# A fused NSA + DSA decoder layer on one Trainium2 core: another price for transfers in the order, own raw buffers for the MLP, one tile for two tables

## The chip, the core and the metric

The kernel runs on one core of a Trainium2 chip. The metric is the device time of one launch in microseconds. Engines are called as the profile calls them: PE (TensorE; PEld is its weight load), DVE (VectorE), ACT (ScalarE), POOL (GpSimd) and SP (SyncE, which here only issues transfers).

## What is computed

One decoder layer over 512 tokens of width 1024, in float32. One projection feeds two groups of heads, which are mixed side by side and mapped back together:

```
h = rms_norm(x, norm_gain)                        # 512 x 1024
q_n, kc, vc, ks, vs, kw, vw, gates, z_n, q_d, k_d, v_d, qi, ki, wi, z_d = split(h @ w_in)
# group A (8 heads, 2 kv heads)
qn, ks, kw = rope(rms_norm(.))                    # per head, width 64
kc_cmp = rope(rms_norm(compress(kc)));  vc_cmp = compress(vc)
   # compress: blocks of 32 tokens, stride 16 -> flat(2048) @ w1(2048 x 256) + b1 -> silu -> @ w2(256 x 64)
o_n = g0*attend(qn, kc_cmp, vc_cmp) + g1*attend(qn, selected blocks of ks, vs) + g2*attend(qn, kw, vw)
# group B (8 heads, 2 kv heads): an indexer picks 128 keys for each query
score = sum_h wi[h] * relu(rope(qi)[h] @ rope(ki)^T)
keep  = top_k(score, 128), causal
o_d   = attend(rope(rms_norm(q_d)), rope(rms_norm(k_d)), v_d) on the kept keys
out   = x + concat(o_n * silu(z_n), o_d * silu(z_d)) @ w_out
```

There are two compress MLPs, one for keys and one for values; each has its own `w1` of 2048 x 256.

## The kernel before, in words

**Precision.** A float32 matrix product is made of three products of rounded parts: a weight tile is loaded raw, ACT casts it to its high part and POOL (or DVE) subtracts that from the raw tile for the low part (`split`, L355 to L357). So each weight piece of 256 KB costs a transfer, an ACT cast (L356) and a subtraction (L357), and then PE multiplies high by high, high by low and low by high (L390, L400).

**Raw pieces.** `load_raw` (L349) takes a tile from a ring and issues the transfer on SP (L352). All weights share the ring "raw" of four buffers (`RAWB`), the sixteen pieces of `w1` that `load_w1` (L733) fetches among them; a transfer into a buffer waits until the cast and the subtraction of the piece that held it are done. In names, `raw_w103` is piece 3 of the keys' `w1`, `raw_w110` piece 0 of the values'; `w1h`, `w1l` are their parts. Weights of the projection are B (indexer and small ones), C (compressed keys and values), Q, D and Z.

**Stages.** Projections for blocks of tokens or columns (L390, L400, L479); the indexer (L672 to L706: PE multiplies the four heads' queries of a block of 128 tokens with the keys at L689, into PSUM banks of the tag S, of which there are two; ACT takes the relu in place at L691; DVE adds the heads up at L693 and L695 and finds the largest 128 of a row in sixteen rounds of L700 and L701); the compress MLP (`chunk_C`, and `hidden`: 32 matmuls at L776, then DVE L781, L782 and L784 with ACT's tanh L783 between them; `hid0` is the keys', `hid1` the values'); norms and rope of queries and keys (L531 and L536, with tables from `tables`, L517 to L522); attention, for blocks of 128 tokens from the last to the first (scores L1010, row maximum on DVE L982, exponential on ACT L987, transposes L1029, product with the values L1040; `P_n301` and `s_n301` are of block 3, its first rows); the gates, and the output product (L1219).

**What sets the order.** The program is written as interleaved generators, but the engines' queues are not in that order. `set_order` (L98) reads all instructions, works out who depends on whom (ring buffers too), gives every one a cost (L115) and every hand-over between engines a latency (`LATENCY`, L71), and lists each engine's queue anew: `turns` runs through the program backward for due times and forward for an order, eight rounds long, and the best order by its own clock is fixed as a chain per engine. So the five queues run strictly in the order that this gives, SP's too. Numbers that steer it: `SOON` (how far ahead an instruction may be waited for that is more urgent), `PORT` (weight of the port that DVE and POOL share, when it is late), `SPARE` (added to the latency of every hand-over to PE) and the price of a transfer (L272 to L282). When a transfer is priced in the forward run, it lands 650 after its issue or when the transfer before is done, whichever is later, and its length (128 partitions times the bytes of a row, by 360) after that.

Of the kernel before, what the change touches and what calls it, by code (L numbers as in the profile page):

```python
# [9 lines left out]
F32 = mybir.dt.float32  # L10
# [6 lines left out]
S, D, HD = 512, 1024, 64  # L17
NT = S // 128
# [65 lines left out]
    ("SP", "PE"): 900, ("SP", "DVE"): 950, ("SP", "Activation"): 900, ("SP", "Pool"): 950,  # L84
}

URGENT, SOON = 3000, 300
PE_URGENT, PE_SOON = 200, 60
ROUNDS = 8

# [2 lines left out]
LO_DVE = {"C": range(2)}  # L93

WBUFS = 4
PORT = 10

TURN = {"Activation": 125, "DVE": 118}  # L98

CHOICE = 0.0  # L100

SPARE = 200

HURRY = {}

# [3 lines left out]
def set_order(tc):  # L109
# [66 lines left out]
    for k, i in enumerate(insts):  # L176
        acc = []
        for w, ap in aps(i):
# [4 lines left out]
            end = off + sum((n - 1) * st for st, n in dims[1:] if st > 0) + 1  # L183
# [17 lines left out]
    for bufs, names in ring.values():  # L201
        names.sort(key=lambda name: int(name.rsplit("_", 1)[1]))
        for x, name in enumerate(names):
# [3 lines left out]
            if x:  # L207
                j = used[names[x - 1]][0]
# [11 lines left out]
    costs = [cost(i, e) for i, e in zip(insts, eng)]  # L220
# [9 lines left out]
    def turns(due, back=False):  # L230
# [5 lines left out]
        idle = defaultdict(float)  # L236
# [13 lines left out]
        for _ in range(count):  # L250
# [21 lines left out]
            end = idle[e] = start[k] + costs[k][0] + more  # L272
            if port[k]:
                idle["port"] = end
            if by[k] == "SP":
                if back:
                    idle["transfers"] = max(idle["transfers"], start[k]) + costs[k][1]
                    end = max(end, idle["transfers"]) + 650
                else:
                    end = max(end + 650, idle["transfers"]) + costs[k][1]  # L280
                    idle["transfers"] = end
                    there = there[1:] + [end + 900]  # L282
            if back:
# [2 lines left out]
            for q in to[k]:  # L286
                left[q] -= 1
                j, i = (q, k) if back else (k, q)
# [20 lines left out]
def tile_hybrid_layer(ctx, tc, xT, x, ng, win, gains, peT, w1, b1, w2, wout, cst, out):  # L309
# [39 lines left out]
    def load_raw(src, shape, name, where=None):  # L349
        tag, bufs = where or ("raw", RAWB)  # L350
        v = wp.tile(shape, F32, tag=tag, name=name, bufs=bufs)
        nc.sync.dma_start(v, src)  # L352
        return v
# [162 lines left out]

    def tables(j, name):  # L517
        gn = gns[:, j, None, :]
        c, s = (work.tile([128, NT, HD], F32, tag="tab" + x, name="tab" + x, bufs=3) for x in "cs")
        nc.gpsimd.tensor_tensor(c, cosd, gn[:, :, :HD].to_broadcast([128, NT, HD]), op=ALU.mult)  # L520
        nc.gpsimd.tensor_tensor(s, sind, gn[:, :, HD:].to_broadcast([128, NT, HD]), op=ALU.mult)
        return c, s  # L522
# [209 lines left out]

    def load_w1(kv):  # L733
        for j in range(8):
            raw = load_raw(w1[:, kv, 2 * j:2 * j + 2, :], [128, 2, 256], f"raw_w1{kv}{j}")
            if j % 2 == 0:
                pair = [w1_tile(kv, j, x) for x in range(2)]
            w1t[kv, j] = [v[:, 2 * (j % 2):2 * (j % 2) + 2] for v in pair]
            split(raw, *w1t[kv, j], nc.gpsimd)
# [659 lines left out]
```

## Time and profile before

| | us |
|---|---|
| three runs: median (lowest, highest) | 316.26 (315.95, 316.64) |
| the profiled execution: its time | 316.42 |
| the profiled execution: span of the core | 314.6 |
| busy in that span: PE, PEld | 306.6, 258.9 |
| busy in that span: DVE, ACT, POOL | 261.1, 242.3, 234.1 |

The span runs from the first to the last instruction that the profile shows; 1.8 us of the profiled execution lie outside of it. The granted clock of PE is 1.00 in all stretches, which is the upper of its two levels, 2.4 GHz. All durations below are of this one profiled execution. Busy time of PE counts a matmul up to its modelled end, and matmuls overlap, so the time that PE loses is read from the starts of its instructions and not from its share.

### The profile page before, as it was taken

The numbers are of one execution on the slowest core, as the hardware profiler recorded it, in microseconds if no ns is written. First come the engines' busy times: TensorE is split into PE (matmuls) and PEld (weight loads), VectorE is DVE, ScalarE is ACT, GpSimd is POOL, SyncE is SP. The second block draws the span as 40 slices with busy tenths as digits, with TensorE's granted clock in tenths as the row PEclk, the third lists the DMA queues.
The fourth block names the chain that finished last, engine by engine and source line by source line (L and its number), as shares of the span: only waits on it lengthen the run. The fifth ranks groups of instructions, "written<-read, shape, count | busy, mean of one in ns | idle before, by whom it ended". The sixth has DMA issues, their size and how long they took to land.

```text
span 314.6 us, 6043 instructions
## 1 busy us (share of the span) xinstructions
PE 306.6 (97%) x1681; PEld 258.9 (82%) x1681; DVE 261.1 (83%) x797; ACT 242.3 (77%) x794; POOL 234.1 (74%) x416
## 2 busy tenths in 40 slices
PE   8999999899999999999999999999999999999995
PEld 5998888789877888888887888888888888888885
DVE  4996624689999999999999999999999999886501
ACT  5971666778999899899999989883379998996500
POOL 2079989799885499995899889766877995667500
PEclk9999999999999999999999999999999999999999
DMA  7990365656510033320040044042435242003011
GB/s 259 417 322 4 98 172 144 173 163 170 165 40 1 0 83 92 97 85 3 3 133 3 4 134 134 2 124 72 135 106 163 70 151 76 20 0 133 2 67 67
DMA packets 21249, 32.16 MB, mean 102 GB/s; under 512 B 5664, under 2 KB 8480, under 8 KB 21216
## 3 DMA queue, kind: packets, MB, share of 16 engines
q1 hardware_dynamic: 21216, 31.78, 33.2%
q8 instruction: 13, 0.21, 0.3%
q14 instruction: 20, 0.16, 0.2%
HBM read 29.04 MB, written 2.47 MB: 100 GB/s over the span
## 4 chain that ended last, share of the span: by engine, by line
PE 81%; ACT 7%; DMA 4%; POOL 3%; issue 2%; DVE 1%; SPq 1%; POOLq 0%; DVEq 0%
PE out L1219 14%; PE z L400 14%; PE D L390 7%; PE on L1040 7%; PE s_n L1010 6%; PE T_n L1029 6%; PE Q L390 5%; PE I L479 5%; DMA raw_w<-in_w_dram 4%; PE C L400 3%; PE od L1040 3%; PE T_d L1029 3%; PE s_d L1010 3%; POOL w1l L357 2%; PE I L443 1%
## 5 line engine op out<-in xcount | busy, mean ns | idle before, releaser
L987 ACT ACTIVATE P_n<-P_n,arena 128x416 f32<-128x416 f32 (+9 forms) x64 | 33.5, 525 | 3.3 <-DVE arena L982 2.8
L1000 POOL TENSOR_SCALAR P_n<-P_n,arena 128x416 f32<-128x416 f32 (+7 forms) x64 | 30.4, 493 | 1.1
L982 DVE CUSTOM_DVE_ANT_0 P_n<-s_n,arena 128x416 f32<-128x416 f32 (+9 forms) x64 | 30.3, 489 | 0.5
L1031 DVE TENSOR_TENSOR ptl<-T_n,pth 128x512 fp32r<-128x512 f32 x40 | 27.4, 684 | 1.8 <-ACT pth L1030 1.3
L1010 PE MATMUL s_n<-kn,arena_r 128*128 128x288 f32 (+12 forms) x116 | 28.3, 328 | 0.5 <-DVE arena_r L621 0.5
L700 DVE MAX8 m<-scores 128x8 f32<-128x512 f32 (+2 forms) x48 | 26.6, 554 | 0.5
L1029 PE MATMUL T_n<-arena,P_n 128*128 128x128 f32 x160 | 26.9, 272 | 0.0
L701 DVE MATCH_REPLACE8 scores<-m,scores 128x512 f32<-128x512 f32 (+2 forms) x48 | 26.1, 544 | 0.1
L400 PE MATMUL z<-hThi,whi_Z 128*128 128x512 f32 x64 | 25.7, 404 | 0.0
L400 PE MATMUL z<-hThi,wlo_Z 128*128 128x512 f32 x64 | 25.3, 398 | 0.0
L400 PE MATMUL z<-hTlo,whi_Z 128*128 128x512 f32 x64 | 25.2, 397 | 0.0
L1030 ACT CAST pth<-T_n 128x512 fp32r<-128x512 f32 x40 | 23.4, 587 | 1.9 <-PE T_n L1029 1.4
L1010 PEld LDWEIGHTS s_n<-kn,arena_r 128*128 128x128 f32 x116 | 20.7, 188 | 4.6 <-DVE arena_r L621 0.7
L1029 PEld LDWEIGHTS T_n<-arena,P_n 128*128 128x128 f32 x160 | 20.3, 140 | 4.8 <-POOL P_n L1000 0.2
L1219 PE MATMUL out<-wohi,mx 128*128 128x512 f32 (+1 forms) x72 | 23.9, 378 | 0.0
L1219 PE MATMUL out<-whi_wo,mx 128*128 128x512 f32 (+1 forms) x72 | 23.6, 379 | 0.0
L357 POOL TENSOR_TENSOR wlo_Z<-raw_Z,whi_Z 128x512 fp32r<-128x512 f32 x16 | 20.4, 1295 | 3.6 <-ACT whi_Z L356 3.5
L390 PE MATMUL Q<-whi_Q,hThi 128*128 128x256 f32 (+1 forms) x64 | 22.4, 349 | 0.0
L357 POOL TENSOR_TENSOR w1l<-raw_w,w1h 128x512 fp32r<-128x512 f32 x16 | 20.5, 1289 | 2.4 <-DMA raw_w<-in_w_dram 1.3
L390 PE MATMUL Q<-whi_Q,hTlo 128*128 128x256 f32 (+1 forms) x64 | 22.2, 347 | 0.0
L390 PE MATMUL Q<-wlo_Q,hThi 128*128 128x256 f32 (+1 forms) x64 | 21.8, 340 | 0.0
L1040 PE MATMUL on<-ptl,arena_r 128*128 128x512 f32 x48 | 20.0, 417 | 0.0
(264 smaller groups left out, 1099.2 us busy)
## 6 DMA issues: line engine op xcount, KB each, us to landing
raw_w<-in_w_dram SPq DMA_DIRECT2D x16, 256.0 KB, 3.1
raw_Z<-in_win_dram SPq DMA_DIRECT2D x16, 256.0 KB, 3.0
wor<-in_wout_dram SPq DMA_DIRECT2D x16, 256.0 KB, 2.8
raw_Q<-in_win_dram SPq DMA_DIRECT2D x12, 256.0 KB, 2.8
raw_D<-in_win_dram SPq DMA_DIRECT2D x8, 256.0 KB, 3.0
xres<-in_x_dram SPq DMA_DIRECT2D x8, 256.0 KB, 2.8
out_dram<-xres SPq DMA_DIRECT2D x7, 256.0 KB, 2.0
xw<-in_xT_dram SPq DMA_DIRECT2D x2, 860.0 KB, 8.8
```

What stands on the lines that cost most here:

```text
L357: engine.tensor_tensor(lo, raw, hi.bitcast(F32), op=ALU.subtract)
L390: nc.tensor.matmul(out_ps, a[:, k, tsl], b, start=(k == 0 and b is hi and a is hT["hi"]), stop=(k == KB - 1 and a is hT["lo"]))
L400: nc.tensor.matmul(out_ps, b[:, csl], a[:, k, :], start=(k == 0 and b is hi and a is hT["hi"]), stop=(k == KB - 1 and b is lo))
L700: nc.vector.max(m8, sc)
L982: nc.vector.tensor_tensor_reduce(P, src_, mask, u.r[:, b:b + 1], 3e38, op0=ALU.add, op1=ALU.min, accum_out=m[:, b:b + 1])
L987: nc.scalar.activation(P, P, AF.Exp, bias=m[:, b:b + 1], scale=-1.0, accum_out=l[:, b:b + 1])
L1000: nc.gpsimd.tensor_scalar(Pb, Pb, l[:, bb:bb + 1], 1.0 if u.gate is not None else 0.5, op0=ALU.mult, op1=ALU.mult)
L1010: nc.tensor.matmul(p, q[0][:, b], k[:, x], start=(x == 0), stop=(x == 1))
L1029: nc.tensor.transpose(p[:, h * 128:(h + 1) * 128], u.P[:, h, j * 128:(j + 1) * 128], ident)
L1031: nc.vector.tensor_tensor(pl, p, ph.bitcast(F32), op=ALU.subtract)
L1040: nc.tensor.matmul(o, u.v[j], pp, start=(u.first and j == 0 and x == 0), stop=(end and x == 1))
L1219: nc.tensor.matmul(p, a, b[:, csl], start=(k == 0 and b is hi and a is mx[0]), stop=(k == 7 and a is mx[1]))
```

## The change

Five places change, and no instruction is added or taken out; each engine has as many as before.

- The forward price of a transfer (L280): where the transfers before are done, it now lands later by 0.7 of its own length.
- `SOON` from 300 to 400, `PORT` from 10 to 8, `SPARE` from 200 to 250.
- The sixteen raw pieces of `w1` get a ring of their own, "raww", of four buffers. The ring "raw" serves the other weights alone.
- The two rope tables of a chunk, two tiles in two rings of three, become the halves of one tile in one ring of three.

```diff
--- before.py
+++ after.py
@@ -84,7 +84,7 @@
     ("SP", "PE"): 900, ("SP", "DVE"): 950, ("SP", "Activation"): 900, ("SP", "Pool"): 950,
 }
 
-URGENT, SOON = 3000, 300
+URGENT, SOON = 3000, 400
 PE_URGENT, PE_SOON = 200, 60
 ROUNDS = 8
 
@@ -93,13 +93,13 @@
 LO_DVE = {"C": range(2)}
 
 WBUFS = 4
-PORT = 10
+PORT = 8
 
 TURN = {"Activation": 125, "DVE": 118}
 
 CHOICE = 0.0
 
-SPARE = 200
+SPARE = 250
 
 HURRY = {}
 
@@ -277,7 +277,7 @@
                     idle["transfers"] = max(idle["transfers"], start[k]) + costs[k][1]
                     end = max(end, idle["transfers"]) + 650
                 else:
-                    end = max(end + 650, idle["transfers"]) + costs[k][1]
+                    end = max(end + 650 + 0.7 * costs[k][1], idle["transfers"]) + costs[k][1]
                     idle["transfers"] = end
                     there = there[1:] + [end + 900]
             if back:
@@ -516,7 +516,8 @@
 
     def tables(j, name):
         gn = gns[:, j, None, :]
-        c, s = (work.tile([128, NT, HD], F32, tag="tab" + x, name="tab" + x, bufs=3) for x in "cs")
+        tab = work.tile([128, 2, NT, HD], F32, tag="tab", name="tab", bufs=3)
+        c, s = tab[:, 0], tab[:, 1]
         nc.gpsimd.tensor_tensor(c, cosd, gn[:, :, :HD].to_broadcast([128, NT, HD]), op=ALU.mult)
         nc.gpsimd.tensor_tensor(s, sind, gn[:, :, HD:].to_broadcast([128, NT, HD]), op=ALU.mult)
         return c, s
@@ -732,7 +733,7 @@
 
     def load_w1(kv):
         for j in range(8):
-            raw = load_raw(w1[:, kv, 2 * j:2 * j + 2, :], [128, 2, 256], f"raw_w1{kv}{j}")
+            raw = load_raw(w1[:, kv, 2 * j:2 * j + 2, :], [128, 2, 256], f"raw_w1{kv}{j}", where=("raww", 4))
             if j % 2 == 0:
                 pair = [w1_tile(kv, j, x) for x in range(2)]
             w1t[kv, j] = [v[:, 2 * (j % 2):2 * (j % 2) + 2] for v in pair]
```

Since the queues follow from the prices and from the buffers, all five are listed anew. Three places, before and after (after the change, lines from the tables on have a number higher by one, L622 for L621).

SP's queue from the last piece of B on, before: the piece of B, three small loads (the MLP's positions, `b1` and `w2`), the eight pieces of the keys' `w1`, then (not shown) pieces of Q.

```order
L352 DMA raw_B7_370<-in_win_dram 128x512
L710 DMA arena_72<-in_peT_dram 128x32
L712 DMA b1r_394<-in_b1_dram 64x512
L714 DMA arena_72<-in_w2_dram 128x256
L352 DMA raw_w100_505<-in_w1_dram 128x512
L352 DMA raw_w101_511<-in_w1_dram 128x512
L352 DMA raw_w102_515<-in_w1_dram 128x512
L352 DMA raw_w103_521<-in_w1_dram 128x512
L352 DMA raw_w104_525<-in_w1_dram 128x512
L352 DMA raw_w105_531<-in_w1_dram 128x512
L352 DMA raw_w106_535<-in_w1_dram 128x512
L352 DMA raw_w107_541<-in_w1_dram 128x512
```

The same place after the change:

```order
L352 DMA raw_B7_370<-in_win_dram 128x512
L352 DMA raw_w100_505<-in_w1_dram 128x512
L352 DMA raw_w101_511<-in_w1_dram 128x512
L352 DMA raw_w102_515<-in_w1_dram 128x512
L352 DMA raw_w103_521<-in_w1_dram 128x512
L713 DMA b1r_394<-in_b1_dram 64x512
L715 DMA arena_72<-in_w2_dram 128x256
L352 DMA raw_w104_525<-in_w1_dram 128x512
L352 DMA raw_Q10_957<-in_win_dram 128x512
L352 DMA raw_Q11_961<-in_win_dram 128x512
L352 DMA raw_w105_531<-in_w1_dram 128x512
L352 DMA raw_Q12_967<-in_win_dram 128x512
```

The first four pieces of `w1` stand straight behind the last piece of B, and the next four alternate with pieces of Q, which now come out of the other ring.

ACT's queue around the indexer of block 3 (`idx30` to `idx33`; `sq` are squares for the norms of projected B, `kix` the indexer's keys, `FS` the MLP's input, L855 a copy of values), before:

```order
L542 ACTIVATE sq_903,ss_kb_547<-B_3_876 128x64
L356 CAST w1h10_1045<-raw_w110_1043 128x512
L764 CAST FS1_495<-ff10_497 128x8x2x31
L542 ACTIVATE sq_910,ss_kb_547<-B_3_876 128x64
L356 CAST w1h10_1045<-raw_w111_1049 128x512
L542 ACTIVATE sq_912,ss_kb_547<-B_3_876 128x64
L691 ACTIVATE idx30_570<-idx30_570 128x512
L691 ACTIVATE idx31_581<-idx31_581 128x512
L356 CAST w1h12_1055<-raw_w112_1053 128x512
L855 ACTIVATE arena_r_73<-B_3_876,arena_72 128x4x64
L356 CAST w1h12_1055<-raw_w113_1059 128x512
L691 ACTIVATE idx32_589<-idx32_589 128x512
```

And after the change:

```order
L543 ACTIVATE sq_899,ss_kb_547<-B_3_874 128x64
L543 ACTIVATE sq_901,ss_kb_547<-B_3_874 128x64
L692 ACTIVATE idx30_568<-idx30_568 128x512
L692 ACTIVATE idx31_579<-idx31_579 128x512
L543 ACTIVATE sq_908,ss_kb_547<-B_3_874 128x64
L356 CAST w1h10_1043<-raw_w110_1041 128x512
L543 ACTIVATE sq_910,ss_kb_547<-B_3_874 128x64
L356 CAST whi_Q20_1081<-raw_Q20_1083 128x512
L692 ACTIVATE idx32_587<-idx32_587 128x512
L356 CAST whi_Q20_1081<-raw_Q21_1087 128x512
L692 ACTIVATE idx33_598<-idx33_598 128x512
```

The first two relus stood behind two casts of the values' `w1`; they now stand ahead of all of them, and one such cast and two of Q's stand between the second and the fourth.

DVE's queue ahead of the first softmax row `P_n301` (MAX and MATCH_REPLACE are rounds of the top-k of block 3, `scr` the MLP of the values, L579 and L621 the transposed keys and queries of the scores), before; straight ahead of these rows stands L784, the last of the three `scr` operations of `hid1`:

```order
L531 TENSOR_TENSOR rt2_1479<-Q2_0_1446,tabs_1124 128x256
L536 TENSOR_TENSOR rt1_1481<-Q2_0_1446,tabc_1123 128x256
L579 TENSOR_TENSOR kn0_397<-kc_ps_1495,kn0_397 64x32
L700 MAX m8_608<-scores_391 128x8
L621 TENSOR_TENSOR arena_r_73<-qT_ps_1521,arena_r_73 64x2x4x32
L579 TENSOR_TENSOR kn1_398<-kc_ps_1495,kn1_398 64x32
L531 TENSOR_TENSOR rt2_1488<-Q2_0_1446,tabs_1443 128x128
L536 TENSOR_TENSOR rt1_1490<-Q2_0_1446,tabc_1442 128x128
L621 TENSOR_TENSOR arena_r_73<-qT_ps_1521,arena_r_73 64x2x4x32
L856 SCALAR_TENSOR_TENSOR arena_r_73<-Q2_0_1446,arena_72,arena_r_73 128x2x64
L701 MATCH_REPLACE scores_391<-m8_608,scores_391 128x512
L982 ISA P_n301_1531,arena_72<-s_n301_1528,arena_72 128x416
```

And after the change, the last twelve rows up to the same instruction:

```order
L537 TENSOR_TENSOR rt1_1477<-Q2_0_1442,tab_1121 128x256
L622 TENSOR_TENSOR arena_r_73<-qT_ps_1517,arena_r_73 64x2x4x32
L580 TENSOR_TENSOR kn1_398<-kc_ps_1491,kn1_398 64x32
L702 MATCH_REPLACE scores_391<-m8_606,scores_391 128x512
L532 TENSOR_TENSOR rt2_1484<-Q2_0_1442,tab_1439 128x128
L537 TENSOR_TENSOR rt1_1486<-Q2_0_1442,tab_1439 128x128
L701 MAX m8_606<-scores_391 128x8
L857 SCALAR_TENSOR_TENSOR arena_r_73<-Q2_0_1442,arena_72,arena_r_73 128x2x64
L702 MATCH_REPLACE scores_391<-m8_606,scores_391 128x512
L701 MAX m8_606<-scores_391 128x8
L702 MATCH_REPLACE scores_391<-m8_606,scores_391 128x512
L983 ISA P_n301_1527,arena_72<-s_n301_1524,arena_72 128x416
```

The three `scr` operations of `hid1` are gone from ahead of this stretch to a place behind the first softmax rows, and thirteen of the sixteen rounds of block 3's top-k stand ahead of `P_n301` where eleven did, three of their MATCH_REPLACE between the second L621 and it where one did.

## Rows read from the trace of the kernel before

**Rows 1.** The page: the span, and busy time with share and count
```profile
span 314.6 us, 6043 instructions
...
PE 306.6 (97%) x1681; PEld 258.9 (82%) x1681; DVE 261.1 (83%) x797; ACT 242.3 (77%) x794; POOL 234.1 (74%) x416
```
**Rows 2.** The chain that ended last: start, us, engine, output, line, count
```profile
212.01 18.79 PE z L400 x82
```
**Rows 3.** Waits of PE, whole span: us in total, times, longest
```profile
PE idx L689 <- DVE scores L695: 2.1, 2, 1.3
...
PE qT_ps L611 <- issue: 0.8, 1, 0.8
PE s_n L1010 <- DVE arena_r L621: 0.5, 1, 0.5
```
**Rows 4.** Timeline of PE: start, us, engine, line, operation, [idle before <-releaser]
```profile
60.78 0.28 PE L390 MATMUL Q<-whi_Q,hTlo 128*128 128x256 f32 x1
62.35 0.73 PE L689 MATMUL idx<-kix,arena_r 128*128 128x512 f32 x2 [1.29 <-DVE scores L695]
62.92 0.28 PE L390 MATMUL Q<-whi_Q,hThi 128*128 128x256 f32 x1
...
70.04 0.28 PE L776 MATMUL hid<-w1h,FS 128*128 128x256 f32 x1
71.09 0.61 PE L689 MATMUL idx<-kix,arena_r 128*128 128x384 f32 x2 [0.78 <-DVE scores L695]
71.55 0.28 PE L776 MATMUL hid<-w1l,FS 128*128 128x256 f32 x1
...
96.28 1.12 PE L1010 MATMUL s_n<-kn,arena_r 128*128 128x448 f32 x4 [0.54 <-DVE arena_r L621]
97.24 0.40 PE L390 MATMUL Q<-whi_Q,hThi 128*128 128x512 f32 x1
```
**Rows 5.** Timeline of ACT around the relus of blocks 3 and 2
```profile
56.11 0.23 ACT L542 ACTIVATE sq<-B 128x64 f32<-128x64 f32 x1
...
57.44 0.62 ACT L356 CAST w1h<-raw_w 128x512 fp32r<-128x512 f32 x1 [1.01 <-DMA raw_w<-in_w_dram]
...
60.07 1.07 ACT L691 ACTIVATE idx<-idx 128x512 f32<-128x512 f32 x2
...
68.46 0.62 ACT L356 CAST w1h<-raw_w 128x512 fp32r<-128x512 f32 x1 [1.24 <-DMA raw_w<-in_w_dram]
...
69.90 0.49 ACT L691 ACTIVATE idx<-idx 128x384 f32<-128x384 f32 x1
```
**Rows 6.** Waits of all engines for one transfer
```profile
ACT w1h L356 <- DMA raw_w<-in_w_dram: 5.6, 8, 1.2
```
**Rows 7.** Timeline of SP: issues in a row, with their count
```profile
10.61 5.00 SPq L352 DMA_DIRECT2D raw_B<-in_win_dram  x4
...
34.60 9.50 SPq L352 DMA_DIRECT2D raw_w<-in_w_dram  x8
...
55.41 10.67 SPq L352 DMA_DIRECT2D raw_w<-in_w_dram  x7
```
**Rows 8.** Timeline of DVE ahead of the first softmax row
```profile
92.56 0.41 DVE L784 SCALAR_TENSOR_TENSOR scr<-hid,scr 64x256 f32<-64x256 f32 x1
...
93.64 0.68 DVE L700 MAX8 m<-scores 128x8 f32<-128x512 f32 x1
...
96.65 0.68 DVE L701 MATCH_REPLACE8 scores<-m,scores 128x512 f32<-128x512 f32 x1
97.25 0.64 DVE L982 CUSTOM_DVE_ANT_0 P_n<-s_n,arena 128x416 f32<-128x416 f32 x1
```
**Rows 9.** Lines: busy us, mean ns of one, idle before and its releasers
```profile
L357 POOL TENSOR_TENSOR w1l<-raw_w,w1h 128x512 fp32r<-128x512 f32 x16 | 20.5, 1289 | 2.4 <-DMA raw_w<-in_w_dram 1.3 <-ACT w1h L356 1.1
```
**Rows 10.** Windows: stretch, us, busy (x) PE PEld DVE ACT POOL, PEclk, DMA, GB/s
```profile
56.50:96.80 40.30, 37.66 (x247) 32.94 (x246) 35.92 (x85) 35.24 (x128) 35.86 (x77) 1.00 0.48 133
96.80:121.50 24.70, 24.70 (x137) 20.76 (x136) 24.09 (x82) 22.80 (x82) 17.19 (x27) 1.00 0.16 44
```

## The prediction

> **What bounds the kernel now.** I read the page's busy times first, then PE's waits, then the chain that ended last, then the timelines where PE waits. PE is busy for 306.6 of 314.6 us [rows 1]. That figure alone proves little, because overlapping matmuls are counted to their modelled ends, so I check it by starts: in the long run of the chain, 82 matmuls of 512 columns take 18.79 us [rows 2], 0.229 us each, and away from four places PE's instructions follow each other at that pace (0.115 us for 256 columns, 0.172 for 384, 0.200 for 448). So the end is set by how much PE has to do and by how long it stands still. It does not get less to do here. What can be gained is the standing still, and the waits of PE say that it is little: 2.1 us in two waits of the indexer, 0.8 for a transpose of queries, 0.5 for the first scores [rows 3]; the rest of the 8.0 us that PE is not busy, 4.6 us, lies at the ends of the span.
>
> By starts, the stalls are these [rows 4]. From 60.78 to 62.92 stand one matmul of 256 columns and two of 512: 2.14 - 0.115 - 0.458 = **1.57 us** lost. From 70.04 to 71.55 stand one of 256 and two of 384: 1.51 - 0.115 - 0.344 = **1.05 us**. At 96.28 PE has been idle for 0.54, and then takes 0.96 for four matmuls of 448 columns that need 0.80: **0.70 us**. I count each with its restart.
>
> **Why PE waits there.** Both indexer matmuls wait for a PSUM bank that DVE's sum L695 reads, and that sum waits for ACT's relu. ACT is in order, and in its queue casts of the values' w1 stand ahead of the relus. Those casts wait for transfers: 1.01 us at 57.44, 1.24 at 68.46, and the relus behind them run at 60.07 and 69.90 [rows 5]. In all ACT loses 5.6 us in eight such waits [rows 6]. The transfers are late because their buffers are: SP issues nothing of w1 until 34.60, 19 us after it has finished issuing B at 15.61, and the second eight only from 55 us on [rows 7]. Casts and subtractions of B hold the four shared buffers until then.
>
> **The change part by part.**
>
> *Own buffers for w1.* In the new order of SP the first four pieces stand straight behind the last of B, and nothing has to be freed for them. They can be issued at some 16 to 20 us instead of 34.60 [rows 7]. The next pieces wait for their own casts and subtractions alone, and pieces of Q no longer stand behind them for a buffer. The issue itself costs PE nothing.
>
> *The relus' new place.* In ACT's new queue the relus of idx30 and idx31 follow two squares of B, of which one ran at 56.11 [rows 5], and no cast of w1 stands between. They then wait for PE's own matmul, so by 57.5 at the latest instead of 60.07. The stall is 1.57 us, and relus that run 2.5 us earlier remove it. Between idx31 and idx33 stand three casts of 0.62 us, two of them of Q. If their transfers are late, the stall returns; Q's pieces are issued well ahead of them in the new SP queue, so I count it as gone. For block 2's relu, at 69.90, the same holds: the cast that waited for 1.24 us at 68.46 is no longer ahead. So -1.57 and -1.05.
>
> *The first scores.* PE waits at 96.28 for the second L621. Ahead of it DVE loses the three operations on hid1, about 0.41 us each [rows 8], 1.2 us in all, and has as many rounds of the top-k as before; and what L621 reads comes earlier by the 2.6 us that PE and ACT have won. So -0.70. The sum of gains is 1.57 + 1.05 + 0.70 = 3.3 us.
>
> *What moves behind.* Nineteen of hid1's 32 matmuls go to a place around the first softmax rows. They are work that PE has to do anyway. But they need late casts and subtractions of w1, which POOL now does close ahead of them; one is 1.29 us [rows 9]. If one of them comes last, PE waits at L777 for a part of that: between 0 and 1.29 us. I take 0.3, nearer to the lower end, since PE's queue has matmuls of other tiles between the pieces, and since such a wait for w1 does not show among PE's waits now [rows 3]. The transfer of the last piece (w117) now stands behind two copies of keys in SP's queue, which belongs to the same bound.
>
> *More rounds ahead of the first softmax row.* Two more rounds of the top-k, 0.68 + 0.68 us each [rows 8], stand ahead of P_n301: 2.7 us more, less the 1.2 us of hid1, so DVE has **1.5 us** more to do by then. DVE is busy for 35.92 of the 40.30 us before, so it has 4.4 us of room, and only behind 96.8 is it full, 24.09 of 24.70 [rows 10]. So I price it at nothing: the rounds fill what DVE waited, and its row starts earlier, not later. Without that cover it costs 1.5.
>
> *The rest.* The price of a transfer and the three constants do nothing on the chip but make this order. One tile for two tables frees both halves together; they are read by two neighbouring operations of DVE, so a buffer comes free some 0.4 us later at most, ahead of POOL work that isn't due: nothing, or some tenths if POOL should wait for it. The wait for the transpose of queries (0.8) lies far behind this place, in the attention, where the queues are almost the old ones; I leave it.
>
> The sum: -3.3 + 0.3 = **-3.0 us**. The profiled execution took 316.42 (314.6 of span and 1.8 around it), which makes 313.4; it stands 0.16 above the median of the three runs, 316.26, which gives **313.2 us**.
>
> **The rivals.**
>
> *No change, 316.2.* DVE sets the pace behind 96.8, and PE's 3 us are given back there as waits for softmax rows. For it: 24.09 of 24.70 us busy [rows 10]. Against it: PE was never idle in that window, 24.70 of 24.70, and it has other work between (projections of Z) which it would draw forward. The price is what is given back, all 3.0: 316.2. The Trainium skill, "Perfetto Trace Analysis", section "Identifying the Most-Contended Engine", takes the engine of the highest occupancy for the bottleneck, to be optimised first, and judges PE's headroom by its weight loads' busy share and not by matmuls. By that rule DVE with 83% comes ahead of PE's 82% and nothing here shortens it: this rival. The trace goes against the rule: PE's starts leave no gaps but those few us, whatever the share of its weight loads. I give the case 0.11.
>
> *The change doesn't do what it says, 315.8.* SP's queue is in order as well: a piece of Q that waits for its buffer holds the w1 pieces behind it, and the casts in front of idx32 and idx33 wait as now. Then the first stall stays in part, the second too, and only the 0.70 of the first scores is gained, less 0.3 of new waits: 316.26 - 0.4 = 315.8. Against it: the first four pieces have no such neighbour. 0.07.
>
> *Slower, 317.7.* DVE's 1.5 us of added work find no room, since its 4.4 us of idle time are waits for PE and ACT that stay where they are. P_n301 then starts at 97.25 + 1.5, DVE is full from there on, and the end comes 1.5 later: 316.26 + 1.5 = 317.7. It decides from the point where the first softmax row starts later than 97.25 in the changed kernel. Against it: everything ahead of that row moves forward by 2.6 us, more than 1.5. 0.15.
>
> **How the numbers follow.** The forecast, 313.2, with its neighbours (one stall gone and not the other, 314.7; more new waits, up to 1.29, 314.2) has 0.67. Its own range is 311.4 to 315: the lower end takes away the transpose's wait too and adds no new one, 316.26 - 3.3 - 0.8 = 312.2, and 0.8 more of the 4.6 us at the ends of the span, which a new listing may shift as well. To hold eight of ten the range has to reach over no change and into the slower case: **311.4 to 317.0**, which leaves out half of the slower case, and little below. A measurement of this kernel can tell 0.2%, 0.63 us. Faster by more than that: the forecast with 0.67 and a part of the case in which the change does half of what it says, 0.05: 0.72. Within: 0.13 (no change, and the rest of that case). Slower: 0.15.
>
> **What would show it.** If I am right: w1 is issued first at 16 to 20 us; ACT has no wait for w1 over 0.6; the first relus of block 3 run before 57.5; PE's 2.1 us for the indexer shrink below 0.6; the first softmax row starts at 95.5 or earlier; PE's 0.8 for the transpose stays; and the 3 us are there at 100 us already and still at the end. I am wrong if PE shows waits over 0.5 at L777 for w1's low parts, if P_n301 starts later than 97.25, or if a gain that is there at 100 us is gone by 170, which would be DVE's pace.

## The result, and the profile of the changed kernel

The changed kernel takes **312.62 us** (median of four, 312.27 to 312.76) against 316.11 for the kernel before, measured beside it: a ratio of 0.9893 with a 95% interval of 0.9869 to 0.9916, some 3.4 us less. The forecast was 313.2. The profiled execution took 312.76, its span is 311.0, 3.6 us less than before. The profile after starts with the page (span; busy time) and PE's waits (us in total, times, longest):

```profile
span 311.0 us, 6033 instructions
...
PE 306.0 (98%) x1681; PEld 258.9 (83%) x1681; DVE 263.0 (85%) x797; ACT 241.0 (78%) x794; POOL 234.6 (75%) x416
...
PE I L443 <- DVE arena L445: 1.4, 1, 1.4
PE kT_ps L591 <- DVE FS L766: 0.4, 1, 0.4
```

All three waits of [rows 3] are gone, the transpose's too; PE is as busy as before (306.0 against 306.6) in a shorter span. The wait of 1.4 us is that at the span's start, which the kernel before has as well. One wait is new, 0.36 us for the transposed indexer keys at 33 us, at a place that I had not named:

```profile
32.05 0.39 PE L400 MATMUL C<-hThi,wlo_C 128*128 128x512 f32 x1
32.80 0.41 PE L591 MATMUL kT_ps<-arena,ridx 128*128 128x128 f32 x2 [0.36 <-DVE FS L766]
32.97 0.48 PE L400 MATMUL C<-hThi,whi_C 128*128 128x512 f32 x1
```

The timelines that answer [rows 7], [rows 5], [rows 4] and [rows 8], of SP, ACT, PE, DVE (start, us, engine, line, operation):

```profile
17.06 3.69 SPq L352 DMA_DIRECT2D raw_w<-in_w_dram  x4
...
39.85 6.71 SPq L352 DMA_DIRECT2D raw_w<-in_w_dram  x6
```
```profile
56.64 1.08 ACT L692 ACTIVATE idx<-idx 128x512 f32<-128x512 f32 x2
```
```profile
58.56 0.63 PE L690 MATMUL idx<-kix,arena_r 128*128 128x512 f32 x2
...
165.78 0.74 PE L1011 MATMUL s_n<-kn,arena_r 128*128 128x512 f32 x2
...
167.16 0.38 PE L612 MATMUL qT_ps<-arena,R_d 128*128 128x128 f32 x2
```
```profile
62.82 0.68 DVE L701 MAX8 m<-scores 128x8 f32<-128x512 f32 x1
...
92.28 0.35 DVE L857 SCALAR_TENSOR_TENSOR arena_r<-Q,arena,arena_r 128x128 fp32r<-128x128 f32 x1 [0.28 <-ACT arena_r L856]
...
94.73 0.64 DVE L983 CUSTOM_DVE_ANT_0 P_n<-s_n,arena 128x416 f32<-128x416 f32 x1
```

w1's first transfer is issued at 17.06 instead of 34.60, no cast of w1 waits for one any more, the relus run at 56.64 instead of 60.07, and PE's products for them follow without a stop. The first softmax row starts at 94.73 instead of 97.25. At 167.16 the transpose of queries waits for nothing. In the kernel before it had waited:

```profile
168.16 0.40 PE L400 MATMUL z<-hThi,whi_Z 128*128 128x512 f32 x1
169.33 0.41 PE L611 MATMUL qT_ps<-arena,R_d 128*128 128x128 f32 x2 [0.78 <-issue]
169.50 0.48 PE L1040 MATMUL on<-pth,arena_r 128*128 128x512 f32 x1
```

All the signs that the prediction listed came, but for the transpose's wait, which was to stay.

So the time is as forecast, to 0.6 us. Whether the reasons are right is what the experiments ask. They came out otherwise in two places: the one tile does something, and the transpose's wait goes too.

### The profile page after: what moved, and what is told of

Same layout as the page of the kernel before. It is cut to its first block, busy times and chain, and to the rows that moved or that the text cites. A ratio compares the mean times of both kernels' runs of the same rounds, so it can differ in the third digit from the quotient of the medians.

```text
span 311.0 us, 6033 instructions
## 1 busy us (share of the span) xinstructions
PE 306.0 (98%) x1681; PEld 258.9 (83%) x1681; DVE 263.0 (85%) x797; ACT 241.0 (78%) x794; POOL 234.6 (75%) x416
## 4 chain that ended last, share of the span: by engine, by line
PE 88%; DVE 7%; issue 1%; ACT 1%; DMA 1%; DVEq 0%; ACTq 0%
PE out L1220 15%; PE z L400 14%; PE Q L390 11%; PE on L1041 7%; PE D L390 7%; PE B L390 6%; PE s_n L1011 6%; PE T_n L1030 6%; PE od L1041 3%; PE T_d L1030 3%; PE s_d L1011 3%; PE hid L777 2%; DVE xsq L471 1%; PE idx L690 1%; PE qT_ps L612 1%
## 5 line engine op out<-in xcount | busy, mean ns | idle before, releaser
L400 PE MATMUL z<-hThi,whi_Z 128*128 128x512 f32 x64 | 26.4, 413 | 0.0
L1030 PE MATMUL T_n<-arena,P_n 128*128 128x128 f32 x160 | 26.0, 272 | 0.0
L988 ACT ACTIVATE P_d<-P_d,arena 128x416 f32<-128x416 f32 (+15 forms) x32 | 16.7, 521 | 5.0 <-DVE arena L983 4.9
```

Of the source, the lines that this page charges most:

```text
L400: nc.tensor.matmul(out_ps, b[:, csl], a[:, k, :], start=(k == 0 and b is hi and a is hT["hi"]), stop=(k == KB - 1 and b is lo))
L988: nc.scalar.activation(P, P, AF.Exp, bias=m[:, b:b + 1], scale=-1.0, accum_out=l[:, b:b + 1])
L1030: nc.tensor.transpose(p[:, h * 128:(h + 1) * 128], u.P[:, h, j * 128:(j + 1) * 128], ident)
```

## The experiments

Twelve kernels, each measured beside the kernel before (315.7 to 315.9 us in these sets); the ratio and its 95% interval say more than the time, as sets differ by some tenths. One of e1's six executions took 1727 us; it is left out of the ratio, and the other five have their median at 312.49. The time of e2, e7, e8 and e9 hangs on whether PE's granted clock fell in an execution, which the last section sets out. Edits shift the lines: L628 of e11 is L621 of the kernel before.

| run | what it is | us | ratio (interval) |
|---|---|---|---|
| (changed kernel) | | 312.62 | 0.9893 (0.9869 to 0.9916) |
| e1 | before + own buffers + one tile | 312.65 | 0.9906 (0.9887 to 0.9925) |
| e2 | before + price + one tile | 316.49 | 1.0007 (0.9984 to 1.0029) |
| e3 | changed, old price | 314.03 | 0.9953 (0.9937 to 0.9969) |
| e4 | changed, old constants | 312.86 | 0.9914 (0.9898 to 0.9930) |
| e5 | changed, two casts ahead of the relus | 314.36 | 0.9964 (0.9948 to 0.9981) |
| e6 | e5, and their transfers late | 315.58 | 1.0002 (0.9989 to 1.0015) |
| e7 | changed, all top-k rounds ahead | 317.98 | 1.0072 (1.0051 to 1.0094) |
| e8 | changed, two rounds moved behind | 315.30 | 1.0003 (0.9987 to 1.0020) |
| e9 | e11, relus ahead of two casts | 317.09 | 1.0050 (1.0031 to 1.0069) |
| e10 | e2, one DVE instruction earlier | 316.11 | 1.0010 (0.9997 to 1.0022) |
| e11 | before + one tile, queues as before | 313.90 | 0.9948 (0.9931 to 0.9965) |
| e12 | e11, old places' waits put back | 314.51 | 0.9966 (0.9950 to 0.9982) |

### Which part of the change does it: e1 to e4

e1, own buffers with the old price and the old constants (the one tile is needed for room: beside two tiles for the tables 1,024 bytes of a partition are missing):

```diff
-            raw = load_raw(w1[:, kv, 2 * j:2 * j + 2, :], [128, 2, 256], f"raw_w1{kv}{j}")
+            raw = load_raw(w1[:, kv, 2 * j:2 * j + 2, :], [128, 2, 256], f"raw_w1{kv}{j}", where=("raww", 4))
...
-        c, s = (work.tile([128, NT, HD], F32, tag="tab" + x, name="tab" + x, bufs=3) for x in "cs")
+        tab = work.tile([128, 2, NT, HD], F32, tag="tab", name="tab", bufs=3)
+        c, s = tab[:, 0], tab[:, 1]
```

> The kernel before with own buffers for w1's raw pieces and the one tile for two tables (without it the tiles do not fit beside the new buffers); price and constants as before. In its order the first relus of the indexer's block 3 already stand ahead of all casts of the values' w1. Theory (the buffers release the transfers, and that moves the casts): 312.6 to 313.8 us, PE's waits for the indexer under 0.6 us. Rival (the new price or the constants do it): 315.5 to 316.5, the 2.1 us of the indexer's waits are there.

e2, the price without the buffers:

```diff
-                    end = max(end + 650, idle["transfers"]) + costs[k][1]
+                    end = max(end + 650 + 0.7 * costs[k][1], idle["transfers"]) + costs[k][1]
...
+        tab = work.tile([128, 2, NT, HD], F32, tag="tab", name="tab", bufs=3)
```

> The kernel before with the new price of a transfer and the one tile for two tables; buffers and constants as before. Theory (buffers): 315.5 to 316.8 us, the casts of w110 and w111 still stand ahead of the relus and wait for their transfers, PE's indexer waits stay at 1.5 to 2.5 us. Rival (the price does it): 312.6 to 314.

e3, the changed kernel with the old price, and e4, with the old constants:

```diff
-                    end = max(end + 650 + 0.7 * costs[k][1], idle["transfers"]) + costs[k][1]
+                    end = max(end + 650, idle["transfers"]) + costs[k][1]
```

> The changed kernel with the old price of a transfer; buffers, tile and constants new. Theory (buffers): 312.2 to 313.6 us, no indexer wait over 0.6. Rival (the price does it): 315.5 to 316.5. The scores' wait and the transpose's wait (0.8 and 1.0 us before, by starts) may come back in either, since the order is listed anew.

```diff
-URGENT, SOON = 3000, 400
+URGENT, SOON = 3000, 300
-PORT = 8
+PORT = 10
-SPARE = 250
+SPARE = 200
```

> The changed kernel with the three old constants; buffers, tile and price new. Theory (buffers): 312.2 to 313.6 us, no indexer wait over 0.6. Rival (the constants, with SPARE's 50 ns more at each hand-over to PE, do it): 315.5 to 316.5, or about 313.6 if they are only what took away the transpose's wait of 1.0 us.

Measured: e1 has the whole gain, e4 too, e3 0.6 points less (0.4 us above its expected range), e2 none. Of the constants, PORT changes nothing at all: with 10 or 8 all five queues are the same, instruction by instruction. So neither price nor constants are needed beside the own buffers and the one tile; which of these two it is, these four cannot tell, as each of them has the one tile. And e2 is not what the theory said of it. With the old ring its w1 is issued early too, first at 20.77 us, its indexer waits are gone as well, and yet its median is that of the kernel before. PE's waits in e2, and DVE's timeline where the long one ends:

```profile
PE Q L390 <- DVE arena_r L857: 2.1, 1, 2.1
```
```profile
97.44 0.71 DVE L983 CUSTOM_DVE_ANT_0 P_n<-s_n,arena 128x480 f32<-128x480 f32 x1
...
98.91 0.34 DVE L857 SCALAR_TENSOR_TENSOR arena_r<-Q,arena,arena_r 128x128 fp32r<-128x128 f32 x1
```

PE, which had won its time earlier, stands for 2.10 us until DVE's L857 (of `Q2_0`) frees the bank of Q. In e2's order it stands behind all four first softmax rows; in the changed kernel it stands ahead of them, as the order shown with the change has it, at 92.28, and so it does in e1, e3, e4 and e11. So this is a matter of one instruction's place. It is the mechanism of the rival "no change", time given back at a release by DVE, though not in the changed kernel. And the windows of e2 (stretch, us, busy of PE, PEld, DVE, ACT, POOL, granted clock) show that the wait cost more than its length:

```profile
97.00:99.30 2.30, 0.21 (x2) 0.00 (x0) 2.30 (x12) 2.30 (x10) 0.46 (x1) 1.00 0.00 0
100.30:103.50 3.20, 3.20 (x10) 2.31 (x9) 3.02 (x8) 2.37 (x12) 2.64 (x5) 0.50 0.00 0
```

Behind it the granted clock is 0.50, the lower level, 1.2 GHz, from 100.3 to 103.5. This is an execution of 317.03 us. In five of e2's twelve the mean clock stayed at 0.999 or more, and those took 314.59 to 315.80, median 314.76, still 1.2 below the kernel before. If the wait is the same in these, it takes back a part of the gain by itself, and the clock behind it the rest in the other seven.

e3 shows how little an early DVE counts for by itself. Its top-k and its first softmax row start later than before the change (65.36 and 97.25), and it is still 1.5 to 1.9 us faster, by the ratio and by the medians:

```profile
65.69 0.69 DVE L701 MAX8 m<-scores 128x8 f32<-128x512 f32 x1
...
98.18 0.64 DVE L983 CUSTOM_DVE_ANT_0 P_n<-s_n,arena 128x416 f32<-128x416 f32 x1
```

### The relus' place and the transfers: e5 and e6

Edits of the changed kernel's queues, after the listing. e5 moves the casts of w110 and w111 on ACT:

```diff
+    l = order["Activation"]
+    moved = [k for k in l if nm(insts[k].ins)[0].startswith(("raw_w110_", "raw_w111_"))]
+    l[:] = [k for k in l if k not in moved]
+    at = min(x for x, k in enumerate(l) if nm(insts[k].outs)[0].startswith("idx30_"))
+    l[at:at] = moved
```

> The changed kernel with one edit of ACT's queue: the casts of w110 and w111, whose transfers have long landed there, stand ahead of the relus of idx30 and idx31 again, as before the change. The relus come two casts later, 56.64 + 1.1 = 57.8 us; PE's fourth product has some 0.6 us to spare. Theory (a cast in front of a relu harms only when it waits for a transfer): PE waits 0.3 to 0.6, time 312.6 to 313.2. Rival (the place in the queue alone does it): PE's 1.5 us come back, 314 or more.

e6 adds a later place on SP for the transfers of w110 to w113:

```diff
+    l = order["SP"]
...
+    at = max(x for x, k in enumerate(l) if nm(insts[k].ins)[0].startswith("dr_gate")) + 1
+    l[at:at] = moved
```

> The same, and SP issues w110 to w113 only behind the copies of the gates, as before the change, at some 54.5 us instead of 40 to 46. Theory: the two casts wait for their transfers until about 58 and 58.6, the relus run at 59.5 instead of 56.64, PE waits 2 to 2.8 us for the indexer's bank, time 314.6 to 315.4, about 2 above the same kernel with the early transfers. Rival (PE's stall hangs on other things of the order): no more than 0.5 above it.

ACT in e5 and in e6, PE's longest wait (besides the start) in each:

```profile
57.68 1.14 ACT L362 CAST w1h<-raw_w 128x512 fp32r<-128x512 f32 x2 [1.07 <-PE hid L783]
58.73 1.06 ACT L698 ACTIVATE idx<-idx 128x512 f32<-128x512 f32 x2
```
```profile
PE Q L396 <- DVE rt L543: 1.4, 1, 1.4
```
```profile
58.84 1.35 ACT L367 CAST w1h<-raw_w 128x512 fp32r<-128x512 f32 x2 [1.97 <-DMA raw_w<-in_w_dram]
```
```profile
PE Q L401 <- DVE rt L548: 1.3, 1, 1.3
```

e5 cost 1.7 us where I had 0.6 at most. The casts, whose transfers had landed, now waited for something else: 1.07 us for PE's products of hid0, which still held the place of w1h. So the relus came at 58.73, 2.1 us late and not 1.1. The rival's time came, 314 or more, though not by its stall at the indexer. In e6 they wait for the transfer, 1.97 us, and the time is 1.2 us longer again, between the theory's 2 and the rival's 0.5. The direction is the theory's, and a cast in front of a relu does harm by what it waits for. But PE doesn't lose the time at the indexer in either: it loses it at 74 to 76 us, 1.4 and 1.3 us, waiting for DVE's rope of Q. That late relus delay DVE, and so its next result for PE, fits this, but no run took it apart. The expected place of the loss was wrong.

### DVE's work around the first softmax row: e7 and e8

e7 moves the last three rounds of the top-k ahead of the row, e8 takes two of the thirteen from ahead of it to behind its rows:

```diff
+    rounds = [k for k in l if "Max" in type(insts[k]).__name__ or "MatchReplace" in type(insts[k]).__name__][:32]
+    at = min(x for x, k in enumerate(l) if nm(insts[k].outs)[0].startswith("P_n301_"))
+    moved = [k for k in l[at:] if k in rounds]
...
```

> The changed kernel with DVE's last three rounds of block 3's top-k moved ahead of the first softmax row: 3 x 1.36 = 4.1 us more in front of it, so it starts at 98.8 instead of 94.73. Theory (DVE's work in front of that row costs nothing as long as PE has other matmuls): PE has some 2 us of them, so 1 to 2.5 us are lost, 313.6 to 315. Rival A (hidden wholly): 312.6. Rival B (DVE sets the pace, all is lost at once): 316.5 or more.

```diff
...
+    moved = rounds[22:26]
+    l[:] = [k for k in l if k not in moved]
+    at = max(x for x, k in enumerate(l) if any(n.startswith("s_n301_") for n in nm(insts[k].ins))) + 1
+    l[at:at] = moved
```

> The changed kernel with two of the thirteen rounds that stand ahead of the first softmax row moved behind its four rows, so that eleven stand ahead as before the change. The row starts up to 2.7 us earlier, 92.3 at the earliest. Theory (the two rounds fill time in which DVE would wait, or in which PE has other work): 312.3 to 313.0, no change. Rival (they cost their 1.5 us): 311.1 to 311.6.

DVE's first softmax row and PE's waits in e7, then in e8:

```profile
99.56 0.64 DVE L990 CUSTOM_DVE_ANT_0 P_n<-s_n,arena 128x416 f32<-128x416 f32 x1
```
```profile
100.71 0.41 PE L619 MATMUL qT_ps<-arena,R_q 128*128 128x128 f32 x2 [0.96 <-DVE arena L990]
...
105.09 0.50 PE L397 MATMUL Q<-whi_Q,hThi 128*128 128x512 f32 x1 [2.22 <-DVE arena_r L864]
```
```profile
94.45 0.65 DVE L990 CUSTOM_DVE_ANT_0 P_n<-s_n,arena 128x416 f32<-128x416 f32 x1 [1.98 <-DMA arena<-dr_q]
```
```profile
102.87 0.50 PE L397 MATMUL Q<-whi_Q,hThi 128*128 128x512 f32 x1 [1.61 <-DVE arena_r L864]
```

Both lose, and neither by the theory's number. In e7 the row starts 4.8 us later than in the changed kernel and the time is 5.4 us longer (3.9 and 4.6 in the two executions whose clock stayed up): rival B, all is lost at once, with PE waiting 0.96 and 2.22 us for banks that DVE frees. In e8 the row can't start earlier than 94.45, since it waits for a transfer (`dr_q`, 1.98 us idle); what stood ahead of it for nothing now stands behind it and costs 2.7 us by the medians (3.5 by the ratios), of which the clock is a part: the seven executions whose clock stayed up have their median at 314.96, 2.3 us above the changed kernel, and the other five at 316.39. The two rounds are 2 x 1.36 = 2.7 us long. So they did stand in a gap, as the prediction had it, and their place there is worth most of their length: behind the rows they stand ahead of the L864 that frees Q's next bank, for which PE then waits 1.61 us.

### The old queues: e9 to e12

e11 has all five queues of the kernel before, instruction by instruction, and the tables in one tile. (The listing is kept by counting the halves of the tile as the two tiles they were.) e9 adds one edit of ACT's queue to it (the casts of w110 and w111 behind the relu of idx31), e10 moves one instruction of DVE's in e2 (`k`, the L857 of `Q2_0`, behind the rope products of its tile):

```diff
-        c, s = (work.tile([128, NT, HD], F32, tag="tab" + x, name="tab" + x, bufs=3) for x in "cs")
+        tab = work.tile([128, 2, NT, HD], F32, tag="tab", name="tab", bufs=3)
+        c, s = tab[:, 0], tab[:, 1]
```

> The kernel before with the two tables in one tile and nothing else, all five queues as they were. Theory: 315.5 to 316.6, no change. Rival (the one tile holds its buffer longer, and POOL waits for it): 316.8 or more.

```diff
+    l = order["Activation"]
...
+    at = max(x for x, k in enumerate(l) if nm(insts[k].outs)[0].startswith("idx31_")) + 1
+    l[at:at] = moved
```

> The kernel before with the one tile for two tables, its queues as they were but for one edit of ACT's: the casts of w110 and w111 stand behind the relus of idx30 and idx31. No own buffers, w1's transfers as late as before. The relus run at 57.9 instead of 60.07. Theory (what counts is when the relus feed DVE): the 1.57 us at 62 are gone, the top-k starts some 2 us earlier than at 65.36, time 1.0 to 1.8 below the same without the edit, 314.3 to 315.1. Rival (the gain needs the early transfers, since the casts that are now behind make POOL and the MLP late): under 0.5 below.

```diff
+    l = order["DVE"]
...
+    l.remove(k)
+    at = max(x for x, q in enumerate(l) if any(n.startswith("Q2_0_") for n in nm(insts[q].ins))) + 1
+    l.insert(at, k)
```

> The kernel with the new price alone (316.5 us, PE waits 2.1 us for DVE's L857 at 97 to 99 us and the granted clock is 0.50 from 100.3 to 103), with one instruction of DVE's queue moved: that L857, which frees the PSUM bank of Q, stands directly behind the two rope products of its tile, two softmax rows earlier. Theory (PE had won its 2.6 us there already and gave them back at this one release): the wait shrinks by 1.3 us to under 0.9, the clock stays at 1.00, time 313.5 to 315.2. Rival (DVE as a whole sets the pace there): the wait comes back at the next release, 316 or more.

e11 was meant to show that the one tile does nothing, and gained 1.9 us. SP's timeline, ACT's relus and PE's waits in it:

```profile
21.32 16.73 SPq L358 DMA_DIRECT2D raw_w<-in_w_dram  x8
...
53.51 4.88 SPq L358 DMA_DIRECT2D raw_w<-in_w_dram  x7
```
```profile
57.93 1.07 ACT L698 ACTIVATE idx<-idx 128x512 f32<-128x512 f32 x2
```
```profile
PE qT_ps L618 <- issue: 0.8, 1, 0.8
PE s_n L1017 <- DVE arena_r L628: 0.5, 1, 0.5
```

With the same queue and the same ring of four, SP issues w1 at 21.32 instead of 34.60, and both indexer waits are gone; the transpose's and the scores' are there as before. The compiled programs show why. All tiles are placed in SBUF by a packer, by how long each lives, and a transfer waits on the chip for whoever used its bytes before. With other tiles the places differ (byte of a partition; what the SP instruction waits for):

```
               before                                 one tile (e11)
raw_B4         210880                                 211392
raw_w100       210880, waits for POOL (raw_B4)        207936, waits for ACT and DVE (xw3, long done)
raw_B5         212928                                 213440
raw_w101       212928, waits for POOL (raw_B5)        219584, waits for nothing before it there
```

In the kernel before, w100 to w103 happened to lie where B4 to B7 lay, whose subtractions end on POOL at 34 to 38 us. In e11 they lie elsewhere. From B4 to the last piece of Q, the pieces of the ring "raw" lie in five places before and in eight in e11, though the ring has four buffers in both. So what held w1 were places, not the number of buffers. e12 tests that: e11, with the same places and queues and the waits put back.

```diff
+    for late, held in (("w100", "B4"), ("w101", "B5"), ("w102", "B6"), ("w103", "B7"),
+                       ("w104", "w100"), ("w105", "w101"), ("w106", "w102"), ("w107", "w103"),
+                       ("Q10", "w104"), ("Q11", "w105"), ("Q12", "w106"), ("w110", "w107")):
+        tc.add_manual_dep(insts[issue[late]], insts[low[held]].name, mybir.DependencyInfo(
+            mybir.DependencyClass.Sync, mybir.DependencyReason.DATA), reason="held")
```

> The one-tile kernel of the run before (313.9 us; queues as in the kernel before, and w1's first transfers at 21.3 us instead of 34.6, because the tiles were placed anew in SBUF and raw_w100 to raw_w103 no longer lie where raw_B4 to raw_B7 lay), with the same places and queues, and the waits that the old places made put back by hand: w100 to w103 wait for the subtractions of B4 to B7, w104 to w107 for those of w100 to w103, Q10 to Q12 and w110 for those of w104 to w107. Theory (the places set the waits, and the waits the 2 us): first issue of w1 at 34 to 35 us, w110 at 54 or later, PE's indexer waits back at 1.5 to 2.6, time 315.5 to 316.8. Rival (the one tile frees something else, for DVE or POOL): 313.5 to 314.5.

```profile
34.19 9.56 SPq L369 DMA_DIRECT2D raw_w<-in_w_dram  x8
...
53.08 0.38 SPq L369 DMA_DIRECT2D raw_w<-in_w_dram  x1
...
54.03 4.74 SPq L369 DMA_DIRECT2D raw_w<-in_w_dram  x7
```
```profile
58.15 0.62 ACT L373 CAST w1h<-raw_w 128x512 fp32r<-128x512 f32 x1 [0.44 <-DMA raw_w<-in_w_dram]
...
58.88 1.07 ACT L709 ACTIVATE idx<-idx 128x512 f32<-128x512 f32 x2
```
```profile
60.77 0.28 PE L407 MATMUL Q<-whi_Q,hTlo 128*128 128x256 f32 x1
61.16 0.73 PE L707 MATMUL idx<-kix,arena_r 128*128 128x512 f32 x2
61.74 0.28 PE L407 MATMUL Q<-whi_Q,hThi 128*128 128x256 f32 x1
```

Half an answer. The first issue of w1 is late again, 34.19, a cast waits for its transfer again (0.44), and PE's first stall is back in part: from 60.77 to 61.74, 0.97 - 0.115 - 0.458 = 0.40 us, by the reckoning of the prediction. The time, 314.51, is 0.6 us above e11, with intervals that overlap, and not the 2 of the theory; it lies at the edge of the rival's range. Two things were not put back: w110 is issued at 53.08 and not at 54.41, and the second pieces of the values' w1, which the second stall hung on, are issued in 4.74 us as in e11 and not in the 10.67 of [rows 7]; in the kernel before, w111 to w113 lie where Q10 to Q12 lay and wait for those subtractions, and e12 doesn't hold them. They are the likely rest, but no run shows it. Shown is that the places set when w1 is issued; that this is the whole of e11's 1.9 us is not.

Taken together, three kernels with the same queues give a series: relus at 57.93, 58.88 and 60.07 (e11, e12, before), first indexer stall 0, 0.40 and 1.57 us. From some 58.5 on, each microsecond of a late relu is one of PE (1.19 us later, 1.17 more of stall, between e12 and the kernel before).

e9 was to gain 1.0 to 1.8 us and is 3.2 us slower than e11, its base. Its premise had gone with e11: w1 is issued early there, the relus run at 57.93 and no stall at 62 is left to be won. What it tests is the edit alone:

```profile
PE kT_ps L605 <- ACT kb_raw L576: 1.8, 1, 1.8
```
```profile
POOL w1l L369 <- ACT w1h L368: 2.8, 1, 2.8
ACT kb_raw L576 <- POOL ny L435: 2.1, 1, 2.1
```

With the casts behind the relus, POOL's subtraction, next in its own queue, waits 2.8 us for the cast, what stands behind it on POOL is late, ACT waits 2.1 us for one of these, and PE waits 1.8 us for ACT, before the transposes of keys at 81. The rival was right. A relu put first on ACT alone is no gain; the new listing moved POOL's work along with it. In e10 the wait that it aimed at shrank from 2.1 to 0.8 us and the clock stayed at 1.00, but another of 1.3 came behind it, for POOL's softmax:

```profile
PE T_n L1037 <- POOL P_n L1008: 1.3, 1, 1.3
PE Q L397 <- DVE arena_r L864: 0.8, 1, 0.8
```

Its 316.11 against e2's 316.49 is no difference that these runs can tell, and against e2's five executions whose clock stayed up (median 314.76) it is no gain at all: e10's clock stayed up in all twelve. The expected 313.5 to 315.2 was missed, and the rival, a wait that comes back at the next release, came.

## Why the prediction was right, point by point

That the sum came out is in part luck: the end of the indexer's stalls was put down to the own buffers, and the one tile, priced at nothing, brings it by itself.

**The indexer's stalls, -1.57 and -1.05.** Gone, as said, by the chain that was named: w1's transfers, casts, relus, DVE's sums, PE. The series of e11, e12 and before bears out the first; the second is only seen to be gone. What was wrong is where the lateness came from. "Casts and subtractions of B hold the four shared buffers" is true of the kernel before only because the packer had put those tiles on the same bytes; e11 has the same ring of four buffers and is free of it. So a transfer here doesn't wait for the ring, as the kernel's description says, but for its bytes. The step that failed is **"the one tile frees both halves together: nothing"**. It is the part that, alone and with no instruction moved, gives 1.9 us, about half of the gain. The diff can't show it, and I did not look at the places. What the own buffers would give without the one tile no run can show, since that doesn't fit.

**The first scores, -0.70.** Gone. It belongs to the new listing: e9, e11 and e12, with the old queues, still have it, e1 to e4 don't.

**The transpose's wait, left in at 0.8.** Gone, also by the listing (there in e9, e11 and e12, in none of e1 to e4 and not in the changed kernel). Between the scores of 512 columns and the transpose PE now has a product, a transpose and two matmuls of Z, where one matmul stood. But that isn't the reason, since in e1 one matmul stands there as before, and the transpose doesn't wait:

```profile
165.03 0.39 PE L400 MATMUL z<-hThi,whi_Z 128*128 128x512 f32 x1
165.26 0.38 PE L612 MATMUL qT_ps<-arena,R_d 128*128 128x128 f32 x2
```

The profile names no releaser for the old wait ("issue"), so what it waited for stays open. "The queues are almost the old ones" was too coarse for it. This is the mis-sized term of the sum: by starts, from 168.16 to 169.50, 1.34 - 0.229 - 0.115 = 1.0 us more.

**New waits, +0.3.** Measured 0.36 idle, and 0.92 - 0.229 - 0.115 = 0.58 by starts (32.05 to 32.97), but at the indexer's keys at 33 us and not at L777, where hid1's late pieces cost PE nothing. Size right, place wrong.

The ledger by starts: 1.57 + 1.05 + 0.70 + 1.0 - 0.58 = 3.7 us, against 3.6 between the spans. The forecast missed the transpose's 1.0 on one side and undersized the new wait on the other. Split by cause: the indexer's two stalls go with the places (e11), the scores' and the transpose's with the new listing, which in e1 comes of the own buffers and in e2 of the price.

**Two more rounds ahead of the softmax row, nothing.** Right: they stand in DVE's wait for `dr_q`, 1.98 us in e8. Undersized in the other direction: behind the rows they cost 2.3 us with the clock up, most of their 2.7.

**The rival "no change".** It did not come, but its mechanism is real: e2 gives back at DVE's release, and by the clock behind it, what PE had won, and e7 and e8 lose about what DVE is late. The reason that I gave against it, that PE "has other work between which it would draw forward", is wrong: PE's queue is fixed and draws nothing forward. As far as the runs tell, the changed kernel escapes since the L857 that frees Q's bank stands ahead of the first softmax rows in its order and behind them in e2's, not since PE had cover; that DVE is earlier (its top-k starts at 62.82) isn't needed, as e3 shows. The Trainium skill, "Perfetto Trace Analysis", section "Identifying the Most-Contended Engine", which would have the engine of the highest occupancy optimised first, is nearer to e7 and e8 than I allowed: in the changed kernel's stretch from 95 to 105 us DVE is busy for 9.39 of 10.00 and PEld for 8.30, where the whole span's shares are close (85% and 83%). But the change itself gained 3.4 us with DVE busier than before (263.0 against 261.1), which goes against it.

**The rival "slower"** decided at a first softmax row later than 97.25. In e7 it is at 99.56, and that kernel is slower than before, by 0.7%. But the sign doesn't decide: in e3 it is at 98.18, and that kernel is faster than before, by 0.5%.

Open: why e3, with own buffers, no wait over 0.2 us in PE's list but the start's and a softmax row at 98.18, is 1.4 us behind the changed kernel, and what of e11's gain hangs on which later transfer.

## What to carry to other kernels

Where a packer places tiles by their lives, a transfer waits for the last user of its bytes, whatever the number of buffers says. Any change of a tile's shape can move those waits, so compare the places and the issue times before an edit of tiles is priced at nothing. And a stall removed on the bound engine is worth its length only if the next release that it waits for isn't later in another engine's queue: PE kept its gain where DVE's L857 stood ahead of the first softmax rows (the changed kernel, e1, e3, e4, e11), and lost it where the new order put that one instruction behind them (e2). An earlier start of DVE's top-k alone doesn't tell these apart: it is at 62.82 in the changed kernel, at 65.69 in e3 and at 65.88 in e2.

## What the runs showed of the chip beyond that

The granted clock of PE fell to 0.50 after waits that were not long. In the profiled executions it did so behind a wait of 2.10 us in e2 (from 100.3 to 103.5 us) and behind one of 1.61 us in e8 (104.5 to 107.8), while behind 2.22 us in e7 and 1.85 us in e9 it stayed at 1.00. These are single executions, though. The mean clock of each execution is on record, and it splits these four kernels in two:

| run | mean clock 0.999 or more: executions, us, median | 0.993 to 0.995: executions, us, median |
|---|---|---|
| e2 | 5, 314.59 to 315.80, 314.76 | 7, 316.46 to 317.24, 317.03 |
| e7 | 2, 316.48 and 317.18 | 4, 317.64 to 318.39, 318.36 |
| e8 | 7, 314.60 to 315.36, 314.96 | 5, 315.71 to 316.96, 316.39 |
| e9 | 5, 316.64 to 317.43, 317.00 | 1, 318.31 |

So the same queues with the same waits lose the clock in some executions and not in others, and where they do, the time is 1.3 to 2.3 us longer. In all executions of the other kernels, whose longest wait of PE is 1.4 us in the profile, the mean is 0.998 or more. A wait of 1.6 to 2.2 us may so cost PE about twice its length, and which execution pays for it these runs don't tell. The windows of e8, then of e7:

```profile
104.50:107.80 3.30, 3.30 (x13) 2.76 (x12) 2.04 (x6) 1.64 (x10) 1.57 (x4) 0.50 0.00 0
```
```profile
103.00:105.60 2.60, 0.50 (x1) 0.19 (x1) 2.46 (x11) 2.58 (x11) 1.26 (x4) 1.00 0.00 0
105.60:109.00 3.40, 3.34 (x19) 2.83 (x20) 3.30 (x11) 3.21 (x14) 2.54 (x6) 1.00 0.00 0
```
